# Output steps of ssm and mlstm in three overlapping parts with stated places in all queues; s5 scan of layer 1 behind both units of mlstm inputs

## The chip, the cores and the metric

One core of one Trainium2 chip runs the whole program. The metric is the device time of one execution in microseconds. The engines are TensorE (PE, matmuls; PEld is its weight load), VectorE (DVE), ScalarE (ACT), GpSimd (POOL) and SyncE (SP, which issues all transfers here). Each takes its instructions in the order in which they were queued at build time, and an instruction whose inputs are not there holds up what stands behind it in the same queue.

## The reference

The reference is a two-layer backbone on a context of 256 tokens and a latent of 256 tokens, width 1024, float32. Each layer is: SwiGLU block, a mixing stage, SwiGLU block, each behind a root-mean-square norm with shift and scale. The mixing stage projects the tokens with one wide matrix and feeds four branches. Two of them matter here, and a third gives way to them:

```python
def ssd_scan(xs, dt, bm, cm, a, h0):            # "ssm", 8 heads, chunks of 128, two directions
    decay = jnp.exp(masked_diff(g, False))      # g: cumulative sum of dt*a in a chunk
    scores = einsum('bcihn,bcjhn->bchij', cq, bq) * decay
    y_intra = einsum('bchij,bcjhp->bcihp', scores, x*dt)
    y_inter = einsum('bcihn,bcih,bchnp->bcihp', cq, exp(g), h_prev)
    return y_intra + y_inter
def mlstm_scan(q, k, v, ig, lf, state):         # "ml", 4 heads, two directions
    w_intra = exp(dmat - m_out) * einsum('bcihk,bcjhk->bchij', qq, kq)
    num = w_intra @ v + w_x * (q @ c_prev)
    den = max(|sum(w_intra) + w_x * (q @ n_prev)|, exp(-m_out))
    return num / den
# "s5": a complex diagonal recurrence over time; "gdn": a gated delta rule with a triangular inverse per chunk
# merge: sum over branches of gate * (y @ w_branch), then @ w_out
```

Layer 0 needs outputs for both segments (four chunks of 128 tokens), layer 1 for the latent alone (two chunks, 2 and 3), though its states run over all four.

## The kernel before, in words

Matmuls of the projections run in three passes of a split weight. `weights` (L360) loads a tile of 512 KB on SP's queue (`w_dma`), ACT casts it to the high part (L366, `w_cast`), DVE forms the low part (L371, `w_split`); the float tile, the high part and the low part have three buffers each. `proj` (L384) runs the three matmuls of a product (L380, L381, L382): a projection of 256 output columns over 512 tokens is two weight tiles and 48 matmuls; over 256 tokens the matmuls have half as many columns. This is called a unit below.

The mixing stage `mix` takes its steps from a string, `MIX_ORDER` (L1708), one per layer. Steps that are one unit of projection: `q0 q2 v0 v1` (inputs of ml), `c0` to `c6` (inputs of ssm), `i0` to `i10` (inputs of gdn), `oM`, `zS`, `zG` (gates of ml, ssm and gdn), `ga1` to `gd3` (merge gates; branch 0 is ssm, 1 ml, 2 s5, 3 gdn). `rows`, `ml`, `ssm`, `s5` and `gdn` are generators; `ssm:1` runs one part, up to its next `yield`. The units between the parts give PE work while other engines prepare.

The order of instructions in each queue is found by a planner at build time, which follows data dependences, buffers and its own estimate of durations. The string sets its preferences, and a mark sets a lower bound: with `'` the step's PE instructions come behind the last matmul of the steps traced before; with `!` its instructions come behind that matmul, behind the last weight cast on ACT, the last split on DVE and the last weight load on SP:

```python
f, behind = f.lstrip("'!"), {"'": 1, "!": 4}.get(f[0], 0)
for h in (self.last_mm, self.w_cast, self.w_split, self.w_dma)[:behind]:
    st.enter_context(self.tc.issue_after(h.ins))
```

The string is taken apart at L1782 and the marks are read at L1849. Before, nearly all output parts of ml and ssm have the mark `'`.

`ssm` (L846): transposes, then a part with the chunk states, then one part per chunk, then the final norm. A chunk takes each direction in turn: SP loads the row tile (`spread`, L742: 8 rows of `rowd` to all 128 partitions, 512 KB); ACT (L910) and DVE (L912) form the differences; ACT takes the Exp (L914, L916); DVE multiplies by the masked scores (L918, L923) and POOL by the C inputs (L925); PE runs the products (L930), and DVE adds the skip (L934). The row tile and E sit in buffer slots 8 and 0, one per direction.

`ml` (L958): load and transposes, states, then one part per chunk, then the norm. A chunk loads 16 rows (1 MB) into slot 7, clamps eight of them on DVE (L1014), takes Exp on ACT (L1015), scores on PE (L1021), masks and weighs on DVE (L1027, L1030, L1036), and runs the products on PE (L1042, L1047); DVE and ACT divide (L1050 to L1058).

`s5_scan` (L1593): U is loaded from `dU` by eight transfers (L1555), PE forms the inputs of the recurrence (L1606), ACT and DVE lay them out (L1614, L1615), and POOL runs 63 steps of four instructions each (L1620 to L1623). `s5` later reads the result (first product L1662). `gdn`'s inverse is a loop of 31 steps on DVE and POOL (L1114, L1116); PE's first matmul after it is L1150.

Of the kernel before, what the change touches and what calls it, by code (L numbers as in the profile page):

```python
# [747 lines left out]
class Ssm:  # L748
# [97 lines left out]
    def ssm(self, l, P, G, o0, dz):  # L846
# [45 lines left out]
        yield  # L892

        y = xs
        for c in range(o0, 4):
# [2 lines left out]
            for g in range(2):
                nc.tensor.matmul(pS[:, g * 128:(g + 1) * 128], lhsT=bc[:, g, sl], rhs=bc[:, 2 + g, sl], start=True, stop=True)
            py = self.ps()  # L900
            nj = sum(1 + ((d, c) in Hs) for d in range(2))
            j = 0
            for d in range(2):
                eg = self.t8((8, 0)[d], [128, 2, 8, 128])
                E, gb = eg[:, 0], eg[:, 1]
                self.spread(gb, d * 8, 8, c)
                for h in range(8):
                    g = G["g"][:, c, d, h:h + 1]
                    if h < 4:
                        nc.scalar.activation(E[:, h], gb[:, h], AF.Relu, scale=-1.0, bias=g)  # L910
                    else:
                        ts(E[:, h], gb[:, h], g, 0.0, op0=OP.subtract, op1=OP.min)  # L912
                inter = (d, c) in Hs
                nc.scalar.activation(E[:, 0:4], E[:, 0:4], AF.Exp, scale=-1.0)  # L914
                e_ = eg.rearrange("p t h i -> p (t h) i")[:, 4:8 + 8 * inter]
                nc.scalar.activation(e_, e_, AF.Exp)  # L916
                Sm, xd = self.k2([128, 2, 128]), self.k2([128, 8, 64])
                tt(Sm, pS[:, 0:256].rearrange("p (g i) -> p g i", g=2),  # L918
                   self.tri[:, d].unsqueeze(1).to_broadcast([128, 2, 128]), op=OP.mult)
                tt(xd, xt[:, c], b8(G["dt"][:, c, d], 64), op=OP.mult)  # L920
                for g in range(2):
                    hs = slice(g * 4, g * 4 + 4)
                    tt(E[:, hs], E[:, hs], Sm[:, g].unsqueeze(1).to_broadcast([128, 4, 128]), op=OP.mult)  # L923
                    if inter:
                        nc.gpsimd.tensor_tensor(gb[:, hs], gb[:, hs], bc[:, 2 + g, sl].unsqueeze(1).to_broadcast([128, 4, 128]), op=OP.mult)  # L925
# [1037 lines left out]
```

## Time and profile before

| | us |
|---|---|
| median of three runs | 2853.37 (2846.23 to 2858.15) |
| the profiled execution | 2849.91 |
| its span, first to last instruction | 2848.2 |
| PE busy | 2710.5 (95%) |
| DVE busy | 1724.6 (61%) |
| ACT busy | 1110.8 (39%) |
| POOL busy | 730.6 (26%) |

The profile is one execution. Busy time is the time in which an engine runs an instruction; idle time before an instruction is put down to what released it last. The granted clock is 1.00 at 2.4 GHz and 0.50 at 1.2 GHz; a stretch that saw both has a mean in between. The mixing stage of layer 0 lies at about 480 to 1240 us of the span, that of layer 1 at about 2080 to 2640.

### The profile page before, as it was taken

How to read it: one execution, taken by the hardware profiler on the slowest of the kernel's cores; microseconds unless marked ns; L12 is line 12 of the kernel's file. 1: busy time of each engine (PE TensorE's matmuls, PEld its weight loads, DVE VectorE, ACT ScalarE, POOL GpSimd, SP SyncE). 2: the span in 40 equal slices, each digit the busy share in tenths (PEclk: the TensorE clock that was granted, in tenths of full speed). 3: DMA queues.
4: the chain of work that ended last, by engine and by line, in shares of the span. 5: the costliest groups of instructions: out<-in, count | busy, mean ns of one | idle time of the engine just before them, and what ended most of it. 6: DMA issues, size and time to landing. Idle time of an engine off the chain costs nothing.

```text
span 2848.2 us, 46282 instructions
## 1 busy us (share of the span) xinstructions
PE 2710.5 (95%) x17710; PEld 2278.2 (80%) x17710; DVE 1724.6 (61%) x3234; ACT 1110.8 (39%) x1711; POOL 730.6 (26%) x1129
## 2 busy tenths in 40 slices
PE   7999999898989999999999999999989998969999
PEld 5777679687867888897678897778978878869999
DVE  6664346477965665674333476554565996766655
ACT  4322224444544533242212353222445456623443
POOL 1442001493021331520000014420107901434100
PEclk9999999999998999999999999999999998979999
DMA  8444878555555544667662353443475557754564
GB/s 269 121 152 132 272 271 216 145 158 153 178 155 174 165 132 152 207 204 260 228 225 89 110 158 121 134 151 106 145 192 168 167 185 237 223 153 129 168 189 144
DMA packets 509819, 494.18 MB, mean 174 GB/s; under 512 B 79380, under 2 KB 437838, under 8 KB 508574
## 3 DMA queue, kind: packets, MB, share of 16 engines
q1 hardware_dynamic: 509598, 491.22, 56.2%
q8 instruction: 140, 2.29, 0.3%
q14 instruction: 81, 0.66, 0.1%
HBM read 429.17 MB, written 61.96 MB: 172 GB/s over the span
## 4 chain that ended last, share of the span: by engine, by line
PE 79%; DVE 6%; DMA 6%; issue 3%; ACT 2%; POOL 2%; SPq 1%; DVEq 0%; POOLq 0%; ACTq 0%
PE ffn.pb L380 15%; PE ffn.pb L381 15%; PE ffn.pb L382 15%; PE gates.pb L381 2%; PE gates.pb L380 2%; PE gates.pb L382 2%; PE ffn.ps L187 2%; DMA ssm.t<-rows.rowd 2%; PE merge.pb L380 1%; PE merge.pb L381 1%; PE merge.pb L382 1%; PE gdnin.pb L382 1%; PE gdnin.pb L381 1%; PE gdnin.pb L380 1%; PE mlin.pb L452 1%
## 5 line engine op out<-in xcount | busy, mean ns | idle before, releaser
L371 DVE TENSOR_TENSOR ffn.wl<-ffn.wf,ffn.wh 128x1024 fp32r<-128x1024 f32 (+1 forms) x308 | 370.3, 1202 | 377.4 <-ACT ffn.wh L366 367.5
L366 ACT CAST ffn.wh<-ffn.wf 128x1024 fp32r<-128x1024 f32 (+1 forms) x308 | 310.4, 1008 | 556.0 <-PE ffn.pb L382 398.6
L382 PE MATMUL ffn.pb<-ffn.t,ffn.wh 128*128 128x256 f32 (+1 forms) x1312 | 438.5, 336 | 0.0
L381 PE MATMUL ffn.pb<-ffn.t,ffn.wl 128*128 128x256 f32 (+1 forms) x1312 | 438.3, 336 | 0.0
L380 PE MATMUL ffn.pb<-ffn.t,ffn.wh 128*128 128x256 f32 (+1 forms) x1312 | 434.7, 338 | 1.0 <-ACT ffn.t L344 1.0
L380 PEld LDWEIGHTS ffn.pb<-ffn.t,ffn.wh 128*128 128x128 f32 x1312 | 244.1, 189 | 34.2 <-ACT ffn.wh L366 4.2
L382 PEld LDWEIGHTS ffn.pb<-ffn.t,ffn.wh 128*128 128x128 f32 x1312 | 246.5, 188 | 29.8 <-issue 2.4
L381 PEld LDWEIGHTS ffn.pb<-ffn.t,ffn.wl 128*128 128x128 f32 x1312 | 247.3, 189 | 28.3 <-issue 1.6
L380 PE MATMUL ffn.pb<-wout.t,ffn.wh 128*128 128x256 f32 (+1 forms) x720 | 242.5, 338 | 0.9 <-ACT wout.t L344 0.9
L381 PE MATMUL ffn.pb<-wout.t,ffn.wl 128*128 128x256 f32 (+1 forms) x720 | 241.4, 336 | 0.0
L382 PE MATMUL ffn.pb<-wout.t,ffn.wh 128*128 128x256 f32 (+1 forms) x720 | 239.2, 335 | 0.0
L381 PE MATMUL gates.pb<-ffn.t,gates.wl 128*128 128x512 f32 (+1 forms) x512 | 178.8, 350 | 5.7 <-DVE gates.wl L371 5.7
L380 PE MATMUL gates.pb<-ffn.t,gates.wh 128*128 128x512 f32 (+1 forms) x512 | 177.1, 348 | 1.9 <-ACT zs.kf L807 1.8
L382 PE MATMUL gates.pb<-ffn.t,gates.wh 128*128 128x512 f32 (+1 forms) x512 | 176.5, 346 | 0.0
L313 POOL TENSOR_TENSOR norm.kf<-norm.kf,norm.kf 128x256 f32<-128x256 f32 x45 | 41.5, 923 | 518.8 <-ACT norm.kf L311 508.4
L380 PEld LDWEIGHTS ffn.pb<-wout.t,ffn.wh 128*128 128x128 f32 x720 | 137.5, 191 | 26.5 <-ACT ffn.wh L366 7.5
L381 PEld LDWEIGHTS ffn.pb<-wout.t,ffn.wl 128*128 128x128 f32 x720 | 136.1, 189 | 16.2 <-issue 0.8
L382 PEld LDWEIGHTS ffn.pb<-wout.t,ffn.wh 128*128 128x128 f32 x720 | 135.1, 189 | 16.0 <-issue 0.8
L380 PE MATMUL ffn.pb<-t,ffn.wh 128*128 128x512 f32 x352 | 142.2, 404 | 2.1 <-DVE ffn.kf L493 1.9
L381 PE MATMUL ffn.pb<-t,ffn.wl 128*128 128x512 f32 x352 | 142.1, 404 | 0.0
L382 PE MATMUL ffn.pb<-t,ffn.wh 128*128 128x512 f32 x352 | 139.3, 401 | 0.0
L381 PEld LDWEIGHTS gates.pb<-ffn.t,gates.wl 128*128 128x128 f32 x512 | 99.8, 195 | 17.9 <-DVE gates.wl L371 6.3
(583 smaller groups left out, 6279.4 us busy)
## 6 DMA issues: line engine op xcount, KB each, us to landing
ffn.wf<-in_ffn_up_dram SPq DMA_DIRECT2D x176, 512.0 KB
ffn.t<-in_ada_w_dram SPq DMA_DIRECT2D x68, 1024.0 KB
ffn.wf<-in_ffn_down_dram SPq DMA_DIRECT2D x104, 512.0 KB
gates.wf<-in_w_in_dram SPq DMA_DIRECT2D x64, 512.0 KB
merge.wf<-in_w_branch_dram SPq DMA_DIRECT2D x32, 512.0 KB
zs.wf<-in_w_in_dram SPq DMA_DIRECT2D x24, 512.0 KB
gdnin.wf<-in_w_in_dram SPq DMA_DIRECT2D x24, 512.0 KB
wout.wf<-in_w_out_dram SPq DMA_DIRECT2D x24, 512.0 KB
```

The source lines that it names most:

```text
L187: nc.tensor.matmul(pm[32 * k:32 * k + 32, :], lhsT=self.sF[:, h * 4 + k, 28 - 4 * i:60 - 4 * i], rhs=ws[h][:, k], start=(h == 0), stop=(h ...
L313: nc.gpsimd.tensor_tensor(sq[0], sq[0], q, op=OP.add)
L366: self.w_cast = nc.scalar.copy(wh[:, :nk, :nw], wf[:, :nk, :nw])
L371: self.w_split = nc.vector.tensor_tensor(wl[:, :nk, :nw], wf[:, :nk, :nw], wh[:, :nk, :nw].bitcast(F32), op=OP.subtract)
L380: mm(out, lhsT=ah, rhs=bh, start=start, stop=False)
L381: mm(out, lhsT=al, rhs=bh, start=False, stop=False)
L382: self.last_mm = mm(out, lhsT=ah, rhs=bl, start=False, stop=stop)
L452: self.last_mm = self.nc.tensor.matmul(o, lhsT=a, rhs=b[:, k], start=(k0 + k == 0 and i == 0 and c % 2 == 0), stop=(k0 + k == nK - 1 and i ...
```

## The change

Three edits. In `ssm`, one output run is now one chunk and direction (eight runs in layer 0, four in layer 1). `rows(i)` sends run i's row transfer into slot 8 or 0 in turn, `prepare(i)` does the work of ACT, DVE and POOL and the scores, `products(i)` runs PE's products and, after the second direction, the skip. A part of the generator is `products(i-1)`, `rows(i+1)`, `prepare(i)`; the first two row transfers stand in the part with the states. In `ml` the same split is made by chunk, with the rows in slots 7 and 0 in turn; the weighed queries are written into the row tile itself. In `MIX_ORDER` the output parts of ml and all but the first parts of ssm get the mark `!`, nearly every part has a unit of projection behind it, in layer 0 more of the merge gates stand ahead of `s5` (ssm has four more parts there, and two more in layer 1), and in layer 1 `s5scan` stands behind `q0` in place of in front of it. The diff is cut: the lines that only move are left out where the new function repeats them.

```diff
@@ -889,50 +889,76 @@
                     tt(Hn, Hs[d, c], b8(G["et"][:, c, d, 0:8], 64), op=OP.mult)
                     tt(Hn, Hn, pv, op=OP.add)
                 Hs[d, ORDER[d][i + 1]] = Hn
-        yield
+
 
         y = xs
-        for c in range(o0, 4):
+        runs = [(c, d) for c in range(o0, 4) for d in range(2)]
+        egs, have, ops = {}, {}, {}
+
+        def rows(i):
+            if i < len(runs):
+                c, d = runs[i]
+                egs[i] = self.t8((8, 0)[i % 2], [128, 2, 8, 128])
+                self.spread(egs[i][:, 1], d * 8, 8, c)
+
+        def prepare(i):
+            c, d = runs[i]
             sl = slice(c * 128, (c + 1) * 128)
-            pS = self.ps()
+            eg = egs.pop(i)
+            E, gb = eg[:, 0], eg[:, 1]
+            for h in range(8):
+                g = G["g"][:, c, d, h:h + 1]
+                if h < 4:
+                    nc.scalar.activation(E[:, h], gb[:, h], AF.Relu, scale=-1.0, bias=g)
+                else:
+                    ts(E[:, h], gb[:, h], g, 0.0, op0=OP.subtract, op1=OP.min)
+            inter = (d, c) in Hs
+            nc.scalar.activation(E[:, 0:4], E[:, 0:4], AF.Exp, scale=-1.0)
+            e_ = eg.rearrange("p t h i -> p (t h) i")[:, 4:8 + 8 * inter]
+            nc.scalar.activation(e_, e_, AF.Exp)
+            if d == 0:
+                pS = have["S"] = self.ps()
+                for g in range(2):
+                    nc.tensor.matmul(pS[:, g * 128:(g + 1) * 128], lhsT=bc[:, g, sl], rhs=bc[:, 2 + g, sl], start=True, stop=True)
+            Sm, xd = self.k2([128, 2, 128]), self.k2([128, 8, 64])
+            tt(xd, xt[:, c], b8(G["dt"][:, c, d], 64), op=OP.mult)
+            tt(Sm, have["S"][:, 0:256].rearrange("p (g i) -> p g i", g=2),
+               self.tri[:, d].unsqueeze(1).to_broadcast([128, 2, 128]), op=OP.mult)
             for g in range(2):
...
-            j = 0
-            for d in range(2):
-                eg = self.t8((8, 0)[d], [128, 2, 8, 128])
-                E, gb = eg[:, 0], eg[:, 1]
-                self.spread(gb, d * 8, 8, c)
+                hs = slice(g * 4, g * 4 + 4)
+                tt(E[:, hs], E[:, hs], Sm[:, g].unsqueeze(1).to_broadcast([128, 4, 128]), op=OP.mult)
+                if inter:
+                    nc.gpsimd.tensor_tensor(gb[:, hs], gb[:, hs], bc[:, 2 + g, sl].unsqueeze(1).to_broadcast([128, 4, 128]), op=OP.mult)
+            ops[i] = ((xd, E), (Hs.get((d, c)), gb))[:1 + inter]
+
+        def products(i):
+            c, d = runs[i]
+            sl = slice(c * 128, (c + 1) * 128)
+            if d == 0:
+                have["y"], have["j"] = self.ps(), 0
+            py = have["y"]
+            nj = sum(1 + ((e, c) in Hs) for e in range(2))
+            for a, b in ops.pop(i):
+                j = have["j"]
                 for h in range(8):
...
-                for a, b in ((xd, E), (Hs.get((d, c)), gb))[:1 + inter]:
-                    for h in range(8):
...
+                    k, e = h // 2, h % 2
+
+                    nc.tensor.matmul(py[e * 64:e * 64 + 64, k * 128:(k + 1) * 128], lhsT=a[:, h], rhs=b[:, h],
+                                     start=(j == 0 and k == 0), stop=(j == nj - 1), skip_group_check=True)
+                have["j"] += 1
+            if d:
+                for k in range(4):
+                    stt(y[:, k, sl], xs[:, k, sl], P["ssm_d"][:, k:k + 1], py[:, k * 128:(k + 1) * 128], op0=OP.mult, op1=OP.add)
+        rows(0)
+        rows(1)
+        yield
+        for i in range(len(runs) + 1):
+            if i:
+                products(i - 1)
+                rows(i + 1)
+            if i < len(runs):
+                prepare(i)
+                yield
@@ -1002,12 +1028,19 @@
                     tt(Cn, Cn, pv, op=OP.add)
                 Cp = Cn
                 Cs[d, ORDER[d][i + 1]] = Cn
-        yield
+
+
         h_ = self.t8(6, [128, 4, 4, 128])
         ss = self.keep("mss", [128, 4, 4])
-        for c in range(o0, 4):
+        rws, ops = {}, {}
+
+        def rows(c):
+            if c < 4:
+                rws[c] = self.spread(self.t8((7, 0)[c % 2], [128, 16, 128]), 24, 16, c)
+
+        def prepare(c):
             sl = slice(c * 128, (c + 1) * 128)
-            rw = self.spread(self.t8(7, [128, 16, 128]), 24, 16, c)
...
-            rd = self.k2([128, 2, 4])
-            pns = []
+            ops[c] = []
...
                 w = rw[:, d * 4:d * 4 + 4]
                 tt(w, w, Sm, op=OP.mult)
-                qw = None
                 if (d, c) in Cs:
-                    qw = self.k2([128, 2, 128])
                     for e in range(2):
                         q = slice(e * 64, e * 64 + 64)
-                        tt(qw[q], qk[q, 0:2, sl], rw[q, 8 + d * 4 + e:8 + d * 4 + 4:2], op=OP.mult)
+                        qw = rw[q, 8 + d * 4 + e:8 + d * 4 + 4:2]
+                        tt(qw, qk[q, 0:2, sl], qw, op=OP.mult)
+                ops[c].append((w, rw[:, 8 + d * 4:12 + d * 4] if (d, c) in Cs else None))
+
+        def products(c):
+            rd = self.k2([128, 2, 4])
+            for d, (w, qw) in enumerate(ops.pop(c)):
                 pn = [self.ps() for _ in range(2)]
-                pns.append(pn)
...
-                        nc.tensor.matmul(dst(h), lhsT=qw[q, k], rhs=Cs[d, c][q, k], start=False, stop=True, skip_group_check=True)
+                        nc.tensor.matmul(dst(h), lhsT=qw[q, h], rhs=Cs[d, c][q, k], start=False, stop=True, skip_group_check=True)
...
-            yield
+        rows(o0)
+        rows(o0 + 1)
+        yield
+        for c in range(o0, 5):
+            if c > o0:
+                products(c - 1)
+                rows(c + 1)
+            if c < 4:
+                prepare(c)
+                yield
...
 MIX_ORDER = (
-    "rows:1 load s5in oM0 s5scan rows:1 oM2 loc q2 q0 v0 v1 ml:2 c0 'ml:1 c2 'ml:1 c4 'ml:1 c6 'ml:1 zS0 zS2 'ml:1 i4 "
-    "'ssm:1 i6 'ssm:1 i8 'ssm:1 i10 'ssm:1 i2 'ssm:1 i0 'ssm:1 ga1 'ssm:1 !s5:1 gb1 's5:1 gc1 s5:1 gdn:1 gd1 gdn:1 ga2 "
-    "gdn:6 glu gb2 gc2 gd2 ga0 gb0 gc0 gd0 zG0 zG2 ga3 !gdn:1 gb3 'gdn:6 gc3 gd3 out m1 m2 m3 m0",
-    "load rows:1 s5in q2 s5scan q0 'rows:1 v0 loc v1 oM0 oM2 ml:2 c0 'ml:1 c2 'ml:1 c4 c6 ml:1 zS0 'ssm:1 zS2 i4 'ssm:1 "
-    "i6 'ssm:1 i8 'ssm:1 i10 'ssm:1 !s5:1 i0 i2 's5:1 zG0 s5:1 zG2 gdn:1 ga2 gdn:1 gb2 gdn:6 "
+    "rows:1 load s5in oM0 s5scan rows:1 oM2 loc q2 q0 v0 v1 ml:2 c0 !ml:1 c2 !ml:1 c4 !ml:1 c6 !ml:1 zS0 !ml:1 zS2 "
+    "'ssm:1 i4 'ssm:1 i6 !ssm:1 i8 !ssm:1 i10 !ssm:1 i2 !ssm:1 i0 !ssm:1 ga1 !ssm:1 gb1 !ssm:1 gc1 !ssm:1 gd1 !ssm:1 "
+    "!s5:1 ga2 's5:1 gb2 s5:1 gdn:1 gc2 gdn:1 gd2 gdn:6 ga0 glu gb0 gc0 gd0 zG0 zG2 !gdn:1 ga3 gb3 'gdn:6 gc3 gd3 "
+    "out m1 m2 m3 m0",
+    "load rows:1 s5in q2 q0 s5scan 'rows:1 v0 loc v1 oM0 oM2 ml:2 c0 !ml:1 c2 !ml:1 c4 c6 !ml:1 zS0 'ssm:1 zS2 "
+    "'ssm:1 i4 !ssm:1 i6 !ssm:1 i8 !ssm:1 i10 !ssm:1 i0 !ssm:1 !s5:1 i2 's5:1 zG0 s5:1 zG2 gdn:1 ga2 gdn:1 gb2 gdn:6 "
     "gc2 glu gd2 ga1 gb1 gc1 gd1 ga0 gb0 gc0 gd0 !gdn:1 ga3 gb3 'gdn:6 gc3 gd3 out m2 m1 m3 m0",
 )
```

## Rows read from the trace of the kernel before

**Rows 1.** The page's first table: engine, busy us, share, instructions.

```profile
PE 2710.5 (95%) x17710; PEld 2278.2 (80%) x17710; DVE 1724.6 (61%) x3234; ACT 1110.8 (39%) x1711; POOL 730.6 (26%) x1129
```

**Rows 2.** Stretches 480:1260 and 2060:2680, sum and mean: busy us by engine.

```profile
sum 1400.00, PE 1287.49 PEld 1130.64 DVE 969.57 ACT 638.67 POOL 514.03; mean PE 643.74 PEld 565.32 DVE 484.78 ACT 319.33 POOL 257.01
```

**Rows 3.** PE's timeline, layer 0, q0: start, us, instruction, [idle before <-its end].

```profile
558.24 0.39 PE L381 MATMUL mlin.pb<-ffn.t,mlin.wl 128*128 128x512 f32 x1
558.47 0.40 PE L382 MATMUL mlin.pb<-ffn.t,mlin.wh 128*128 128x512 f32 x1
...
564.02 0.79 PE L380 MATMUL mlin.pb<-ffn.t,mlin.wh 128*128 128x512 f32 x1 [5.15 <-ACT mlin.wh L366]
```

**Rows 4.** ACT's timeline, the same place.

```profile
555.86 1.28 ACT L910 ACTIVATE ssm.t<-ssm.t,rows.gc 128x128 f32<-128x128 f32 x4 [5.08 <-DMA ssm.t<-rows.rowd]
...
562.94 1.03 ACT L366 CAST mlin.wh<-mlin.wf 128x1024 fp32r<-128x1024 f32 x1
```

**Rows 5.** Stretches: length, busy us of PE, PEld, DVE, ACT, POOL; clock, DMA, GB/s.

```profile
560.00:572.00 12.00, 7.51 (x20) 5.63 (x21) 8.64 (x18) 8.93 (x14) 11.21 (x21) 0.72 0.24 69
679.00:691.00 12.00, 5.09 (x24) 4.10 (x23) 10.29 (x22) 3.12 (x4) 2.66 (x2) 0.72 0.56 180
...
2120.00:2140.00 20.00, 12.07 (x222) 11.71 (x222) 12.30 (x28) 7.48 (x18) 2.04 (x6) 0.74 0.79 127
2170.00:2182.00 12.00, 5.92 (x25) 5.42 (x25) 3.70 (x8) 9.87 (x18) 10.82 (x32) 0.72 0.54 173
...
2518.00:2558.00 40.00, 20.88 (x409) 20.34 (x409) 21.60 (x53) 8.31 (x13) 10.84 (x10) 0.57 0.30 84
```

**Rows 6.** Timelines of PE and ACT, layer 1, at the scan and at oM.

```profile
2127.93 0.87 PE L1606 MATMUL s5scan.ps<-s5scan.t,s5scan.t 128*64 128x64 f32 x11 [8.13 <-DMA s5scan.t<-prep.s5K]
...
2169.18 1.28 ACT L910 ACTIVATE ssm.t<-ssm.t,rows.gc 128x128 f32<-128x128 f32 x4 [4.71 <-DMA ssm.t<-rows.rowd]
...
2175.03 0.58 PE L380 MATMUL zs.pb<-ffn.t,zs.wh 128*128 128x256 f32 x1 [5.28 <-ACT zs.wh L366]
```

**Rows 7.** Timelines of SP, DVE, PE around ml's third chunk, layer 0.

```profile
666.47 0.39 SPq L742 DMA_DIRECT2D ml.t<-rows.rowd  x1
...
677.97 0.48 DVE L1014 TENSOR_SCALAR ml.t<-ml.t,rows.gmc 128x128 f32<-128x128 f32 x2 [6.56 <-DMA ml.t<-rows.rowd]
...
686.22 2.07 PE L1042 MATMUL ml.ps<-ml.k,ml.t 128*128 128x130 f32 x8 [6.91 <-issue]
```

**Rows 8.** PE's waits, 800:860: instruction, releaser: us in total, times, longest.

```profile
PE ssm.ps L930 <- DVE ssm.t L923: 7.5, 8, 1.8
PE ssm.ps L930 <- POOL ssm.t L925: 1.2, 2, 0.8
```

**Rows 9.** PE's waits, 2200:2364, first and last of eight.

```profile
PE zs.pb L381 <- DVE zs.wl L371: 4.5, 2, 2.9
...
PE ml.ps L1070 <- DVE ml.t L1066: 0.6, 1, 0.6
```

**Rows 10.** POOL's timeline, layer 1, ssm's first multiplies.

```profile
2274.01 6.48 POOL L925 TENSOR_TENSOR ssm.t<-ssm.t,ssm.t 128x512 f32<-128x512 f32 x4
```

**Rows 11.** PE's groups by line, 2317.6:2376.6: xcount | busy, mean ns | idle.

```profile
L381 PE MATMUL gates.pb<-ffn.t,gates.wl 128*128 128x256 f32 x38 | 12.9, 338 | 0.0
...
L930 PE MATMUL ssm.ps<-ssm.t,ssm.k 128*64 128x128 f32 x64 | 4.8, 280 | 1.4 <-DVE ssm.t L923 1.4
```

**Rows 12.** Stretches inside the scan of layer 1, columns as in rows 5.

```profile
2160.00:2170.00 10.00, 9.76 (x83) 9.55 (x82) 2.41 (x6) 4.88 (x11) 8.90 (x27) 1.00 0.59 161
2220.00:2230.00 10.00, 10.00 (x59) 8.22 (x58) 9.86 (x21) 5.31 (x11) 9.38 (x16) 1.00 0.61 141
```

**Rows 13.** SP's waits at L742, whole span: durations in ns, min/median/max.

```profile
L742 SPq EVENT_SEMAPHORE  x19: 17/17/1423, 534.8 to 2331.4; - x19
```

**Rows 14.** The chain of waits, 790:860: start, us, piece.

```profile
809.20 8.53 DMA ssm.t<-rows.rowd
```

**Rows 15.** PE's timeline behind the gdn inverse, layer 1.

```profile
2535.42 1.27 PE L1150 MATMUL gdn.ps<-gdn.k,gdn.t 32*32 32x32 f32 x20 [16.78 <-DMA gdn.k<-gdn.gz]
```

More of the change, by code (lines that the diff above doesn't have):

```diff
@@ L891, in ssm @@
                 Hs[d, ORDER[d][i + 1]] = Hn
-        yield
-        y = xs
-        for c in range(o0, 4):
-            sl = slice(c * 128, (c + 1) * 128)
-            pS = self.ps()
[L898 to L901, printed above, removed]
-            j = 0
-            for d in range(2):
-                eg = self.t8((8, 0)[d], [128, 2, 8, 128])
-                E, gb = eg[:, 0], eg[:, 1]
-                self.spread(gb, d * 8, 8, c)
-                for h in range(8):
[L908 to L925, printed above, removed]
-                for a, b in ((xd, E), (Hs.get((d, c)), gb))[:1 + inter]:
-                    for h in range(8):
-                        k, e = h // 2, h % 2
-                        nc.tensor.matmul(py[e * 64:e * 64 + 64, k * 128:(k + 1) * 128], lhsT=a[:, h], rhs=b[:, h],
-                                         start=(j == 0 and k == 0), stop=(j == nj - 1), skip_group_check=True)
-                    j += 1
-            for k in range(4):
-                stt(y[:, k, sl], xs[:, k, sl], P["ssm_d"][:, k:k + 1], py[:, k * 128:(k + 1) * 128], op0=OP.mult, op1=OP.add)
-            yield
@@ new lines, in ssm @@
+        y = xs
+        runs = [(c, d) for c in range(o0, 4) for d in range(2)]
[28 more added lines that the diff above has]
+               self.tri[:, d].unsqueeze(1).to_broadcast([128, 2, 128]), op=OP.mult)
+            for g in range(2):
+                hs = slice(g * 4, g * 4 + 4)
[3 more added lines that the diff above has]
+            ops[i] = ((xd, E), (Hs.get((d, c)), gb))[:1 + inter]
@@ new lines, in products @@
+        def products(i):
+            c, d = runs[i]
+            sl = slice(c * 128, (c + 1) * 128)
+            if d == 0:
[4 more added lines that the diff above has]
+                j = have["j"]
+                for h in range(8):
+                    k, e = h // 2, h % 2
[5 more added lines that the diff above has]
+                    stt(y[:, k, sl], xs[:, k, sl], P["ssm_d"][:, k:k + 1], py[:, k * 128:(k + 1) * 128], op0=OP.mult, op1=OP.add)
@@ L1004, in ml @@
                 Cs[d, ORDER[d][i + 1]] = Cn
-        yield
         h_ = self.t8(6, [128, 4, 4, 128])
         ss = self.keep("mss", [128, 4, 4])
-        for c in range(o0, 4):
+        rws, ops = {}, {}
[3 more added lines that the diff above has]
+        def prepare(c):
             sl = slice(c * 128, (c + 1) * 128)
-            rw = self.spread(self.t8(7, [128, 16, 128]), 24, 16, c)
+            rw = rws.pop(c)
             for d in range(2):
```

## The prediction

> **What bounds the kernel now.** The table of engines comes first: TensorE (PE) is busy for 95% of the span [rows 1]. A change that takes no matmul away can only win what PE idles or runs at its lower clock. The table of stretches over the two mixing stages, the only code the diff touches, says how much that is: of 1400 us PE is busy for 1287.5, so 112.5 us are idle; the next engine, VectorE, is busy for 969.6 [rows 2]. The list of PE's waits and the timelines then say which of these belong to edited steps.
>
> The most telling one: PE stops for 5.15 us until ScalarE (ACT) has cast a weight tile [rows 3]. ACT's timeline shows why. ACT stood 5.08 us at a Relu of the state-space step, for a transfer from `rowd`, and the cast came only after that step's Exp [rows 4]. The state-space output step was hoisted there, in front of the mLSTM step, because its place was stated in PE's queue alone. After such a stop the granted clock falls to 1.2 GHz: the stretch around it has a mean of 0.72 [rows 5], so 12 x 0.28 = 3.4 us of full-speed work are lost.
>
> **The change, part by part.** Counted in the code, no matmul, elementwise instruction or transfer is added or removed: there are still 12 row transfers for ssm and 6 for ml. What changes is when each may issue.
>
> *Stated places in all queues.* Layer 0's hoisted Relus now stand behind a weight cast of the gdn inputs, so the stop above goes: 5.15 + 3.4 = 8.6 us; I take 8.5, since the same ACT work lands later, beside projections. Layer 1 has the twin: ACT stands 4.71 us at the same Relu and PE 5.28 us at the cast behind it [rows 6], with a mean clock of 0.72 again [rows 5]: 8.7, taken 8.5.
>
> *Row tiles in two buffers, products one unit after their preparation.* Today one buffer holds ml's rows, so the transfer for the next chunk issues only after the products that read the old one. SyncE (SP) issued it at 666.47, VectorE (DVE) stood 6.56 us for it until 677.97, and PE stood 6.91 us for what DVE makes of it [rows 7]. The transfer thus took 11.5 us. A projection unit (48 matmuls, 0.23 us apart [rows 3]) lasts 11.3 us. With two buffers the transfer issues one unit earlier and PE comes to the products one unit later, so this wait has about two units of cover. Worth 6.91 plus half of 12 x 0.28 (the rest of the low clock fell into the wait): 8.6, taken 8.
>
> In ssm of layer 0, PE waits 7.5 + 1.2 = 8.7 us, ten times, for what DVE and GpSimd (POOL) multiply for the step it wants at once [rows 8]. A unit of cover removes these; I take 6, because DVE and ACT still stand at row transfers and may be late once or twice.
>
> *s5scan of layer 1 behind q0.* PE waits 8.13 us for transfers before the scan's matmuls [rows 6]. q0 there has 256 columns, half a unit, so 5.6 us of matmuls slide into the gap. The stretch has a mean clock of 0.74 [rows 5], 5.2 us lost, half of which falls into the wait: 5.6 + 2.6 = 8.2. The weights of q0 must be issued by the same SP queue that is busy with the scan's own transfers, so I take 6.
>
> *The rest of layer 1.* From 2200 to 2364 the wait list has eight rows that sum to 13.6 us, from 4.5 down to 0.6 [rows 9]: splits and casts late behind ml and ssm work. I take 6: part of it is transfers and sums that do not move.
>
> Upper bound 8.6 + 8.7 + 8.6 + 8.7 + 8.2 + 13.6 = 56.4; lower bound, if only the two hoisted Relus go, 17; taken 8.5 + 8.5 + 8 + 6 + 6 + 6 = 43.
>
> *What the change costs.* In layer 1 POOL runs the scan until 2274.01, and only then ssm's first four multiplies, 6.48 us [rows 10]. Before, ssm's products all ran after 2317, behind i8 and i10 [rows 11], so this cost nothing. The places now put i8 and i10 (22.6 us) behind the first products, and layer 1's gains take up to 20 us off: 2317 - 43 = 2274, when POOL is just free and needs 3.2 us for the first pair. I charge 4. It costs more if the scan is slower, and it is slower beside a busy DVE: with DVE busy 2.41 of 10 us POOL runs 27 instructions, with 9.86 it runs 16 [rows 12]. The 252 instructions of a scan (63 steps of four) take 93 us at the one rate and 158 at the other; if all of it moved to the lower one, layer 1's gain would be gone (third rival). The Trainium skill, "SBUF — State Buffer", section "Who interferes with whom", has the rule that speaks against this change: a VectorE instruction with two SBUF inputs and a GpSimd instruction that reads SBUF exclude each other for the whole instruction. The trace agrees, with the 27 against 16 instructions above.
>
> SP: a transfer into a reused buffer waits in SP's queue for the products; behind it stand the weight loads of the next units. The wait before such a transfer was at most 1.4 us [rows 13], and weights have three buffers of half a unit each, so nothing to 14 us over ten such transfers, taken 0. DVE and ACT: behind a Relu or clamp that waits stand the next unit's cast and split. A 512 KB transfer takes 8.5 us [rows 14], less than a unit, so I take 0; the other end is the second rival.
>
> Sum: 43 - 4 = 39 us. The profiled execution took 2849.9 us (span 2848.2 and 1.7 around it), 3.5 below the median of 2853.4; from the median, **2814 us**.
>
> **Rivals.**
>
> 1. *The end of layer 1 is covered as well.* PE waits 16.78 us for the gdn inverse [rows 15], and the mean clock there is 0.57 [rows 5]: 40 x 0.43 = 17 us, of which about 8 fall on work. For: the order text has s5 ahead of all gates, yet 38 x 3 = 114 gate matmuls, 2.4 units, ran before s5's first product [rows 11], since ml and ssm were late. If these steps keep their places, s5 and gdn start earlier against the projections that cover the inverse. Against: DVE runs the inverse as well and splits the same weights. 25 us more: 2789. Chance 0.20.
>
> 2. *Slower: the stated place makes DVE and ACT stand at a row transfer.* Ten transfers cannot be sent before their loop (2 of ml, 6 of ssm in layer 0, 2 of ssm in layer 1). Each is sent when products end, and its reader has a place behind the last cast and split of the next unit, which can run up to half a unit ahead of PE. If the place comes first, everything behind it stalls as in [rows 3]: 5.15 + 3.4 = 8.6 us. Eight times (the ssm ones) are 69: 2814 + 69 = 2883. It outweighs the gain from the fifth such stop on. For: 11.5 us measured for the larger transfer is no less than a unit. Against: ssm's 8.5 is less, and weights already split keep PE going. Chance 0.12. The Trainium skill, "DMA: Bandwidth & Descriptors", section "Bandwidth", gives 6.15 us for 1 MB loaded into 128 partitions from GpSimd's queue, about half of the 11.5 us that the 1 MB row transfer took here. By that figure all ten would be covered and this rival void; the trace disagrees, so it stays.
>
> 3. *Layer 1 hands its part back*, to the scan on POOL or to a longer wait at the inverse. Of 43, the 20.5 of layer 1 go with the 4 charged: 2814 + 16.5 = 2830. For: DVE and POOL, not PE, pace that stretch. Chance 0.13.
>
> 4. *It does not do what it says.* A place is a lower bound and the instruction order between the places is found by a planner, so waits may move by a unit without getting shorter: the 114 matmuls ahead of s5 show how far the real order drifts from the text [rows 11]. 2853. Chance 0.13.
>
> **How the numbers follow.** Forecast 0.42, rivals 0.20, 0.12, 0.13, 0.13. The forecast's own range is 2797 (56.4 of gain) to 2836 (the hoisted Relus alone). From 2775 to 2862 the range holds the forecast, the third and fourth rivals and most of the first; it leaves out the second and a little at each end, some 0.18. A change within 0.5% (14.3 us) is what a measurement here cannot tell from none. Faster: 0.41 + 0.20 + 0.12 = 0.73. Slower: the second rival, 0.12. The same: 0.15.
>
> **What would show it.** PE's waits for `mlin.wh` at layer 0's q0 and for `zs.wh` at layer 1's oM0 are gone, and ACT has no ssm Relu before ml's first chunk. The 6.91 us ahead of ml's products is gone, and ml's clamps wait less for `rowd`. The wait ahead of the scan's matmuls in layer 1 is under 3 us. POOL's first ssm multiply of layer 1 follows the scan without a pause (then the scan is the new bound there); with a pause, the 4 us were not paid. s5's product of layer 1 comes before the gates: then the 16.78 us shrink. I am wrong if PE's idle time in the two stages stays near 112 us, or if casts wait behind ssm Relus inside the ssm stretch.

## The result and the profile after

The changed kernel takes 2810.13 us (median of four runs, 2805.00 to 2820.62) against 2855.76 us for the kernel before beside it: ratio 0.9849, 95% interval 0.9811 to 0.9888. A second set gave 2811.46 against 2850.83: 0.9868, 0.9854 to 0.9883. So it is faster by 1.3 to 1.5%, and 2814 us had been predicted. The profiled execution took 2805.0 us.

The first table of the page after, which answers to [rows 1]:

```profile
PE 2687.4 (96%) x17710; PEld 2258.2 (81%) x17710; DVE 1729.0 (62%) x3234; ACT 1114.1 (40%) x1711; POOL 748.3 (27%) x1129
```

The number of instructions is the same on every engine; PE is busy for 23 us less. Where both come from is seen by cutting each trace at the same work: layer 0's mixing stage from the first matmul of its `rows` step to the last of the output projection, layer 1's from the first matmul of ml's inputs to the last of the output projection. First the kernel before, then the kernel after, in the columns of [rows 5]:

```profile
478.00:1263.00 785.00, 744.06 (x4738) 624.01 (x4738) 519.01 (x1012) 338.24 (x535) 267.03 (x404) 0.97 0.56 166
2103.00:2643.00 540.00, 472.78 (x4097) 439.42 (x4095) 401.03 (x821) 260.33 (x439) 235.79 (x385) 0.92 0.62 181
```

```profile
478.00:1242.00 764.00, 734.48 (x4741) 617.61 (x4741) 524.82 (x1013) 339.84 (x534) 270.02 (x404) 0.98 0.58 170
2082.00:2606.00 524.00, 466.88 (x4098) 433.77 (x4096) 400.74 (x821) 261.62 (x440) 249.79 (x385) 0.93 0.64 186
```

Layer 0 is 21 us shorter: idle time falls from 785 - 744.1 = 40.9 to 29.5 us, and the busy time for the same matmuls by 9.6 us, with the mean clock up from 0.97 to 0.98. Layer 1 is 16 us shorter: 10.1 of idle time and 5.9 of busy time. The part between the two stages took 840.15 us in both. The remaining 7.6 us of the two profiles lie in the last SwiGLU block, which the change does not touch (below).

At layer 0's q0, the place of [rows 3] and [rows 4], the same 40 us before and after:

```profile
550.00:590.00 40.00, 34.38 (x207) 30.19 (x207) 24.55 (x40) 20.60 (x36) 37.02 (x76) 0.91 0.53 156
```

```profile
550.00:590.00 40.00, 40.00 (x272) 36.79 (x271) 25.65 (x43) 16.42 (x24) 37.10 (x75) 1.00 0.68 194
```

PE does 272 matmuls in place of 207, all at full clock. At ml's third chunk, which answers to [rows 7], DVE's clamp of the changed kernel still stands for its rows. PE's next products belong to the second chunk, since products now run one unit late, and wait 1.76 us in place of 6.91; this is the only wait of PE ahead of ml's output products in that layer:

```profile
629.83 0.43 DVE L1047 TENSOR_SCALAR ml.t<-ml.t,rows.gmc 128x128 f32<-128x128 f32 x1 [6.14 <-DMA ml.t<-rows.rowd]
```

```profile
641.10 1.13 PE L1077 MATMUL ml.ps<-ml.k,ml.t 128*128 128x130 f32 x8 [1.76 <-DVE ml.t L1062]
```

Layer 1's gains and its remaining stops show in PE's waits from the start of its stage (waiting instruction, releaser: us in total, times, longest), which answer to [rows 6]:

```profile
PE s5scan.ps L1650 <- DMA s5scan.t<-prep.s5K: 4.6, 1, 4.6
PE zs.pb L380 <- ACT zs.wh L366: 3.1, 1, 3.1
PE ml.ps L1020 <- DVE ml.k L1016: 2.9, 1, 2.9
PE rows.ps L716 <- DVE s5scan.t L1659: 2.2, 1, 2.2
PE zs.pb L381 <- DVE zs.wl L371: 0.9, 1, 0.9
```

8.13 us at the scan have become 4.6, and the stop at oM's cast and split is 3.1 + 0.9 in place of 5.3 + 1.3. ACT's timeline says that it has another cause now: ACT stands for the load of ml's own queries and keys, no longer for ssm's rows.

```profile
2147.21 0.63 ACT L992 ACTIVATE ml.t<-ml.t 128x512 f32<-128x512 f32 x1 [15.10 <-DMA ml.t<-ffn.mlqk]
```

How little that start of the stage gained is seen by cutting layer 1 at the same place and at s5's first product. The kernel before, then the kernel after:

```profile
2103.00:2200.00 97.00, 82.05 (x813) 75.03 (x813) 53.40 (x121) 46.40 (x87) 50.84 (x136) 0.91 0.70 180
2200.00:2376.60 176.60, 162.97 (x1056) 141.38 (x1052) 160.71 (x316) 94.27 (x152) 86.95 (x142) 0.95 0.61 184
```

```profile
2082.00:2180.00 98.00, 84.11 (x840) 76.05 (x839) 55.58 (x130) 43.82 (x79) 51.28 (x132) 0.97 0.73 189
2180.00:2337.70 157.70, 150.33 (x966) 130.58 (x964) 154.01 (x301) 92.69 (x153) 101.72 (x146) 0.95 0.60 181
```

PE idles 15.0 us in the first 97 us of the stage before and 13.9 in the first 98 after; from there to s5's first product it is 13.6 and 7.4.

The wait behind the gdn inverse of [rows 15] is where it was:

```profile
2498.83 3.43 PE L1194 MATMUL gdn.ps<-gdn.k,gdn.t 32*32 32x32 f32 x64 [16.46 <-DMA gdn.k<-gdn.gz]
```

### The profile page after: what moved, and what is told of

Its sections match the earlier page's. It is cut to its first block, busy times and chain, and to the rows that moved or that the text cites. A ratio compares the mean times of both kernels' runs of the same rounds, so it can differ in the third digit from the quotient of the medians.

```text
span 2803.3 us, 46292 instructions
## 1 busy us (share of the span) xinstructions
PE 2687.4 (96%) x17710; PEld 2258.2 (81%) x17710; DVE 1729.0 (62%) x3234; ACT 1114.1 (40%) x1711; POOL 748.3 (27%) x1129
## 4 chain that ended last, share of the span: by engine, by line
PE 50%; DVE 9%; issue 4%; DMA 4%; POOL 2%; ACT 1%; SPq 1%; DVEq 0%; POOLq 0%; ACTq 0%
PE ffn.pb L380 11%; PE ffn.pb L381 11%; PE ffn.pb L382 11%; PE gates.pb L380 2%; PE gates.pb L381 2%; PE gates.pb L382 2%; PE ffn.ps L187 1%; PE merge.pb L382 1%; PE merge.pb L380 1%; PE merge.pb L381 1%; DVE gdnin.kf L790 1%; PE wout.pb L382 1%; PE wout.pb L381 1%; PE wout.pb L380 1%; DVE ssmin.kf L790 1%
## 5 line engine op out<-in xcount | busy, mean ns | idle before, releaser
L493 DVE SCALAR_TENSOR_TENSOR ffn.kf<-ffn.kf,ffn.pb 128x512 f32<-128x512 f32 (+1 forms) x88 | 54.6, 620 | 94.8 <-ACT ffn.kf L491 94.8
```

The source lines that it names most:

```text
L493: nc.vector.scalar_tensor_tensor(g[:, :n], t[:, :n], 1.0, p, op0=OP.add, op1=OP.mult)
```

## The experiments

All lengths are of one profiled execution each, cut as above; "last" is from there to the end of the span.

| kernel | median us | ratio to before (95%) | layer 0 | layer 1 | last |
|---|---|---|---|---|---|
| before | 2855.8 | | 784.7 | 540.1 | 205.1 |
| before, again (e13) | 2852.3 | 1.0000 (0.9986 to 1.0015) | 788.4 | 534.5 | 198.2 |
| changed | 2810.1 | 0.9849 (0.9811 to 0.9888) | 763.3 | 524.1 | 197.5 |
| changed, again (e4) | 2811.5 | 0.9868 (0.9854 to 0.9883) | 766.8 | 525.2 | 197.6 |
| e1: no places | 2827.4 | 0.9920 (0.9904 to 0.9935) | 776.3 | 526.8 | 198.7 |
| e2: places, old code | 2852.6 | 1.0007 (0.9992 to 1.0021) | 785.0 | 546.7 | 197.7 |
| e3: scan first | 2811.9 | 0.9862 (0.9841 to 0.9883) | 770.3 | 524.2 | 198.3 |
| e5: ml alone | 2819.5 | 0.9893 (0.9869 to 0.9917) | 766.7 | 531.5 | 199.0 |
| e6: ssm alone | 2833.4 | 0.9937 (0.9916 to 0.9959) | 778.5 | 534.4 | 198.7 |
| e7: ml behind its gate | 2801.6 | 0.9835 (0.9809 to 0.9860) | 762.6 | 517.2 | 198.4 |
| e9: short scan | 2808.1 | 0.9849 (0.9821 to 0.9878) | 762.2 | 528.4 | 197.6 |
| e10: ssm free | 2821.6 | 0.9895 (0.9878 to 0.9911) | 766.2 | 531.6 | 198.9 |
| e11: ml free | 2829.6 | 0.9918 (0.9901 to 0.9934) | 782.6 | 526.6 | 205.6 |
| e12: ml behind each unit | 2819.7 | 0.9887 (0.9873 to 0.9902) | 766.9 | 532.2 | 198.8 |

The changed kernel, its repeat, e3, e7, e9 and e12 have the same order of steps in layer 0 and lie between 762.2 and 770.3 there. The two profiles of the kernel before differ by 3.7 us in layer 0 and 5.6 in layer 1. A difference of less than some 8 us in layer 0 or 6 us in layer 1 is therefore not read as one, unless a wait in the trace shows it.

**e4, e13: each kernel again.** No edit.

> The changed kernel once more, nothing altered. The last 205 us of the program before (the second SwiGLU block of layer 1, which the change does not touch) took 7.6 us less in the profile of the changed kernel, with the 256-column matmuls 113.3 ns apart in place of 117.8 at the same granted clock of 1.00. Theory P (the pace belongs to the kernel): 197.5 us again there, mixing stages of 763 and 524 us within 1 us. Theory R (the pace is an accident of the execution): the stretch, or another with 256 columns in layer 1, comes out at the other pace, up to 7.6 us away, and the mixing stages move by no more than their own matmuls' pace.

> The kernel before once more. Its profile had 784.7 and 540.1 us in the mixing stages and 205.1 us in the last SwiGLU block, where eight other profiles, one of them of old code, had 197.5 to 199. Theory R (that pace is an accident of one execution): 197.5 to 199 us this time, the mixing stages within 4 us of 784.7 and 540.1. Theory P (the pace belongs to this program): 205 us again.

Theory R held. The kernel before has 198.2 us in its last block the second time, and e11 is the only other one at 205. The rest of the spread is in the stages. In this second pair PE idles 44.8 and then 29.9 us in layer 0, 64.8 and then 54.9 in layer 1, so the gain of idle time is there again. Of the busy time, layer 0 gains again (743.6 to 737.1 us), layer 1 does not (469.7 to 470.4).

**e1: the places taken away.** In every output part of ml and ssm:

```diff
-c0 !ml:1 c2 !ml:1 c4 !ml:1 c6 !ml:1 zS0 !ml:1
+c0 'ml:1 c2 'ml:1 c4 'ml:1 c6 'ml:1 zS0 'ml:1
...
-i6 !ssm:1 i8 !ssm:1 i10 !ssm:1
+i6 'ssm:1 i8 'ssm:1 i10 'ssm:1
```

> The changed kernel with the places of the ml and ssm output parts stated in PE's queue alone again; the two buffers, the lag of one unit and the order of steps stay. Theory A (the places make the hoisted ScalarE work wait its turn): ScalarE's ssm Relus go back in front of the weight casts at layer 0's q0 and at layer 1's oM, PE stops there again for about 5 us each, and with the low clock each mixing stage is 8 to 9 us longer (layer 0 from 763 to about 772, layer 1 from 524 to about 532): about 2827 us. Theory B (the gain comes from the two buffers and the lag; the places are idle): both stages within 2 us of the changed kernel, about 2810 us.

Measured: 2827.43, theory A to the microsecond. But the split over the layers is not A's: layer 0 loses about 11 us and layer 1 about 2, no more than its spread. And the stop at q0 is not a copy of the old one. It ends with VectorE, not with ACT's cast, and ACT stands three times around it, 8.44 us for ml's Exp, 4.48 for ssm's Relu and 5.26 for ml's second Exp, so theory A has only part of the cause:

```profile
566.01 0.79 PE L381 MATMUL mlin.pb<-ffn.t,mlin.wl 128*128 128x512 f32 x1 [5.98 <-DVE mlin.kf L783]
```

In layer 1 PE stops at oM for 6.9 + 2.3 us in place of 3.1 + 0.9, and the stage is still only 2 us longer. Buffers, lag and order alone thus keep 23 of the 39 us that the changed kernel gained beside the same runs of the kernel before (2850.83); the places are worth the other 16. What each of buffers, lag and order is worth was not tested by itself, except for the scan's place (e3).

**e2: the places given to the old code.**

```diff
-c0 'ml:1 c2 'ml:1 c4 'ml:1 c6 'ml:1 zS0 zS2 'ml:1 i4 'ssm:1
+c0 !ml:1 c2 !ml:1 c4 !ml:1 c6 !ml:1 zS0 zS2 !ml:1 i4 !ssm:1
```

> The kernel before with the places of its ml and ssm output parts stated in all four queues, nothing else. Theory A: the two hoisted stops go (8.5 us in each stage: layer 0 from 785 to about 776, layer 1 from 540 to about 531), while the 6.9 us ahead of ml's products and the 8.7 us of ssm's small waits in layer 0 stay: about 2836 us. Theory B: nothing is gained, about 2855 us, since a part that is prepared and used in one step now also starts later. Theory D (places without the lag cost): DVE and ACT do everything for a product only after the unit's casts, PE waits longer at each ml and ssm product, and the kernel is slower than before, 2865 us or more.

Theory A missed by 17 us: nothing was gained. The stop at q0 is gone here too (PE runs its four ml input units in 45.28 us, as in the changed kernel, in place of 53.95), yet the stage is as long as before. PE's waits from 790 to 870 us, next to [rows 8], show where it went:

```profile
PE ssm.ps L930 <- DVE ssm.t L923: 8.7, 8, 2.1
PE ssm.ps L283 <- ACT ssm.k L839: 7.0, 1, 7.0
PE ssm.ps L930 <- POOL ssm.t L925: 3.9, 5, 1.1
```

8.7 us of waits for the operands of a step have become 8.7 + 3.9, and 7.0 more stand ahead of the norm. A part that is prepared and used in one step, and may not start early, is late when PE comes to it. Layer 1 is even longer, 546.7 us against 540.1 and 534.5. So the places gave nothing without the rest of the change; the rest gave 23 us without the places (e1).

**e3: the scan in front of q0 again.**

```diff
-s5in q2 q0 s5scan 'rows:1
+s5in q2 s5scan q0 'rows:1
```

> The changed kernel with layer 1's s5 scan in front of q0 again. Theory A: PE waits about 8.1 us ahead of the scan's matmuls in place of 4.6, and layer 1's mixing stage is 4 to 6 us longer (524 to about 529): about 2815 us. Rival (GpSimd's scan is what bounds ssm there): the scan starts and ends some 5 us earlier, ssm's first multiplies too, and layer 1's stage is the same or shorter: 2805 to 2810 us.

Measured: 2811.93, and 524.2 us in layer 1, as with the scan behind q0. PE's waits at the start of the stage:

```profile
PE s5scan.ps L1650 <- DMA s5scan.t<-prep.s5K: 9.6, 1, 9.6
PE ml.ps L1020 <- DVE ml.k L1016: 3.6, 1, 3.6
PE ssmin.pb L381 <- DVE ssmin.wl L371: 0.8, 1, 0.8
```

The wait at the scan is longer, 9.6 us, but the 3.1 at oM's cast and the 2.2 behind the scan are not there: in the first 98 us of the stage 4.6 + 3.1 + 2.9 + 2.2 + 0.9 = 13.7 stand against 9.6 + 3.6 + 0.8 = 14.0. The stop moved; it was not covered.

**e5 and e6: ml's part alone, ssm's part alone.** Each takes one generator from the change with its places (e6 with layer 0's later order too) and leaves the other, and the scan, as before.

```diff
 e5
-c0 'ml:1 c2 'ml:1 c4 'ml:1 c6 'ml:1 zS0 zS2 'ml:1 i4 'ssm:1
+c0 !ml:1 c2 !ml:1 c4 !ml:1 c6 !ml:1 zS0 !ml:1 zS2 i4 'ssm:1
 e6
-zS2 'ml:1 i4 'ssm:1 i6 'ssm:1 i8 'ssm:1
+zS2 'ml:1 'ssm:1 i4 'ssm:1 i6 !ssm:1 i8 !ssm:1
```

> From the kernel before, ml's part of the change alone: two row buffers, products one unit late, places of ml's parts in all queues; ssm's code, places and order and the scan's place as before. Theory A (the parts add up): ml gives its 8 us of layer 0 (785 to about 777) and 3 to 5 us in layer 1 (540 to about 536), the stop at q0 stays since ssm's Relus are still free to go ahead: about 2840 us. Theory J (the parts work only together, as the places without the lag gave nothing): under 4 us in all, about 2848 us.

> From the kernel before, ssm's part of the change alone: one chunk and direction per part, products one unit late, places in all queues, layer 0's later order; ml and the scan's place as before. Theory A (the parts add up): the stop at layer 0's q0 and its twin in layer 1 go, and the small waits of ssm too: layer 0 from 785 to about 772, layer 1 from 540 to about 529: about 2826 us. Theory J: under 8 us in all, about 2843 us or more.

ml alone gives 30 us, over twice what theory A had for it, and 18 to 22 of them in layer 0: within the spread, the whole of that layer's gain. ssm alone gives 16 us. The two sum to 46 us and both take away the stop at q0, so their gains overlap; it counts once in the whole. The stop is absent in both; the same 40 us as above, e5 and then e6:

```profile
550.00:590.00 40.00, 40.00 (x273) 36.77 (x272) 26.58 (x44) 18.57 (x30) 37.17 (x73) 1.00 0.64 189
```

```profile
550.00:590.00 40.00, 40.00 (x259) 36.19 (x258) 26.16 (x44) 17.27 (x26) 37.18 (x73) 1.00 0.66 194
```

In e5 ssm's Relu still goes ahead on ACT and stands there for 9.41 us, and PE does not stop; in e6 it is ml's Exp, which stands for 7.84 us. The line of e5:

```profile
552.88 1.29 ACT L910 ACTIVATE ssm.t<-ssm.t,rows.gc 128x128 f32<-128x128 f32 x4 [9.41 <-DMA ssm.t<-rows.rowd]
```

The twin in layer 1 parts the two. In e5 it is gone, with ssm's Relu standing 7.64 us on ACT. In e6, where ssm's Relus have their place, it stays, and ACT stands twice for ml (PE's waits at oM, then ACT's timeline ahead of the casts):

```profile
PE zs.pb L380 <- ACT zs.wh L366: 6.3, 1, 6.3
PE zs.pb L381 <- DVE zs.wl L371: 0.7, 1, 0.7
```

```profile
2155.30 1.06 ACT L1041 ACTIVATE ml.t<-ml.t 128x1024 f32<-128x1024 f32 x1 [9.06 <-DVE ml.t L1040]
...
2168.31 0.63 ACT L992 ACTIVATE ml.t<-ml.t 128x512 f32<-128x512 f32 x1 [8.95 <-DMA ml.t<-ffn.mlqk]
```

**e10 and e11: one of the two freed in the changed kernel.** The marks of ssm (e10) or of ml (e11) are `'` again, as in e1.

> The changed kernel with the places of the ssm output parts stated in PE's queue alone; ml's stay in all queues. Without any of these places layer 0's stage took 776 us, with all of them 763 to 770. Theory A (as predicted: the hoisted ssm Relus on ScalarE stop PE at q0): PE stops about 5 us at q0 again, layer 0's stage about 775 us, layer 1's 527: about 2825 us. Theory M (ml's clamps on VectorE and Exp on ScalarE, waiting there for their own rows, make the stop; the ssm Relu alone is covered by weights already split, as with ml's part alone, where ScalarE stood 9.41 us for it and PE ran on): no stop at q0, layer 0's stage within 763 to 771 us: about 2812 us.

> The changed kernel with the places of the ml output parts stated in PE's queue alone; ssm's stay in all queues. Theory A: no stop at q0, since the ssm Relus keep their place: 763 to 771 us in layer 0's stage, about 2812 us. Theory M: the stop of 5 to 6 us at q0 is back, with VectorE standing at ml's clamps for the second chunk's rows, and layer 0's stage takes about 775 us: about 2823 us.

Theory M held for layer 0, though e11's stage is longer still than its 775 us (782.6; the four ml input units took 54.7 us in place of 45.3). PE's 40 us at q0, e10 and then e11:

```profile
550.00:590.00 40.00, 40.00 (x272) 36.74 (x271) 24.30 (x37) 18.58 (x30) 37.10 (x75) 1.00 0.72 200
```

```profile
550.00:590.00 40.00, 33.39 (x179) 28.57 (x178) 24.51 (x48) 15.13 (x21) 36.86 (x82) 0.87 0.52 159
```

In e10 ACT stands 9.31 us for ssm's rows, ahead of a cast, and the casts and splits already done carry PE over it. In e11 no ssm work stands ahead; ml's does. Its clamps wait on DVE and its Exp behind them on ACT, twice, since two row buffers let the second chunk come forward as well (DVE, then ACT):

```profile
567.78 1.99 DVE L1047 TENSOR_SCALAR ml.t<-ml.t,rows.gmc 128x128 f32<-128x128 f32 x8 [12.16 <-issue]
569.69 1.34 DVE L371 TENSOR_TENSOR mlin.wl<-mlin.wf,mlin.wh 128x1024 fp32r<-128x1024 f32 x1
```

```profile
553.92 1.06 ACT L1048 ACTIVATE ml.t<-ml.t 128x1024 f32<-128x1024 f32 x1 [8.26 <-DVE ml.t L1047]
...
569.81 1.06 ACT L1048 ACTIVATE ml.t<-ml.t 128x1024 f32<-128x1024 f32 x1 [12.43 <-DVE ml.t L1047]
```

The median of e10, 2821.57, is still 10 us above the changed kernel: its layer 1 is 7 us longer, in one profile. That part theory M did not foresee. The traces place it: s5's first product comes 257.0 us after the stage's start, as in the changed kernel (256.0 and 257.7), and from there to the first matmul behind the gdn inverse it is 166.0 us in place of 161.1 and 160.0. What makes that stretch longer stays open.

**e9: half of the scan.** Layer 1's scan runs 31 of its 63 steps; the later half of that recurrence is left out.

```diff
-        for n in range(1, 64):
+        for n in range(1, 32 if l else 64):
```

> The changed kernel with 31 of the 63 steps of layer 1's s5 scan on GpSimd, which leaves the later half of that recurrence out. In the changed kernel the scan runs from 2127 to 2266 and ssm's first multiplies follow it without a pause. Theory S (the scan bounds ssm's output part, and with it all that follows in layer 1, for at least the 4 us charged): the multiplies come 40 us or more earlier and layer 1's stage of 524 us is shorter by 4 to 20 us. Rival (the multiplies have slack, their products have a later place): they come earlier, the products do not, and the stage stays within 2 us of 524. A faster DVE beside a quiet GpSimd would give up to 2 us more in both.

Counted from the start of the stage, POOL ends the scan 83 us earlier, stands for 55 us, and begins ssm's multiplies 28 us earlier. First the last scan instruction and the first multiplies of e9, then the first multiplies of the changed kernel, which follow its scan at once:

```profile
2181.05 0.50 POOL L1667 TENSOR_TENSOR s5scan.t<-s5scan.s5m 128x64 f32<-128x64 f32 x1
2236.68 3.39 POOL L931 TENSOR_TENSOR ssm.t<-ssm.t,ssm.t 128x512 f32<-128x512 f32 x2 [55.13 <-ACT gdnin.wh L366]
```

```profile
2266.17 6.79 POOL L931 TENSOR_TENSOR ssm.t<-ssm.t,ssm.t 128x512 f32<-128x512 f32 x4
```

Layer 1 is not shorter: 528.4 us against 524.1 and 525.2, and s5's first product comes 256.3 us after the stage's start, against 256.0 and 257.7. The length of the scan bounds nothing there.

**e7 and e12: a better order for layer 1.**

```diff
 e7
-oM0 oM2 ml:2 c0 !ml:1 c2 !ml:1 c4 c6 !ml:1
+oM0 !ml:1 oM2 !ml:1 c0 !ml:1 c2 !ml:1 c4 c6 !ml:1
 e12
+oM0 oM2 !ml:1 c0 !ml:1 c2 !ml:1 c4 !ml:1 c6 !ml:1
```

> The changed kernel with layer 1's first two parts of ml given places too: the first behind the first unit of ml's gate, the second behind the second unit. In the changed kernel ScalarE stands 15.10 us there for ml's load from memory ahead of a weight cast, and PE stops 3.13 us. Theory A (same cause as the hoisted Relus): that stop goes and with it some clock, layer 1's stage 3 to 5 us shorter (525 to about 521): about 2807 us. Rival (ml's states are then late): PE waits 3 us or more for ml's first transposes or states in its place, and nothing is gained: 2811 us or more.

> A version meant to beat the changed kernel: in layer 1 each of ml's five parts stands behind one unit (the first behind both units of its gate, then one behind each of the four units of ssm's inputs), all in all queues. Giving the first two parts places one unit earlier took layer 1's stage from 524 to 517 us. Theory A (every part behind its own unit, the loads of ml have a unit more): PE's wait of 3.27 us for ml's values goes too, layer 1's stage 513 to 517 us, about 2799 us. Rival (ml's last part and so ssm's transposes come a unit later, and the chain from ssm to the inverse with them): 520 to 528 us, about 2808 us.

e7 is the fastest of all: 2801.64 us (2798.84 to 2808.39), and layer 1 takes 517.2. It was timed beside the kernel before, not beside the changed one, whose eight runs lie between 2805.00 and 2820.62 us, and the intervals of the two ratios overlap; that it beats that one too rests on the stage, 7 us shorter in one profile, little more than the spread. PE's waits at the start of its stage:

```profile
PE s5scan.ps L1650 <- DMA s5scan.t<-prep.s5K: 5.2, 1, 5.2
PE ml.ps L1020 <- DMA ml.k<-ffn.mlv: 3.3, 1, 3.3
PE rows.ps L716 <- DVE s5scan.t L1659: 2.0, 1, 2.0
```

The wait for oM's cast is gone, 3.1 + 0.9 us, and ACT stands for ml's load for 1.12 us in place of 15.10. Both theories had part of it: a wait of 3.3 for ml's values takes the place, and what is won shows later, in a first s5 product 247.8 us after the stage's start in place of 256.0. That the stop alone was worth 7 us is not shown: e3 is without it too, and e1 has more than twice of it, and their stages are within 3 us of the changed kernel's. e12, one unit later, loses it all and more: 532.2 us, worse than its rival's 520 to 528. PE's last matmul of ml ends there at 171 us of the stage, against 158 in e7, and its first of ssm starts at 182 against 169. Of the 15 us between the two stages 8.5 are there at s5's first product (256.3 us) and 5 more come between it and the inverse.

## Why the prediction was right, and where it was not

**The stop at layer 0's q0, 8.5 us: right size, half the cause.** It went: PE's four ml input units take 45.28 us in place of 53.95, 8.7 less. But "The state-space output step was hoisted there" is not the whole reason. In the kernel before ACT stood twice in a row, for ml's clamped rows and then for ssm's (the second is the line of [rows 4]):

```profile
548.27 1.06 ACT L1015 ACTIVATE ml.t<-ml.t 128x1024 f32<-128x1024 f32 x1 [7.99 <-DVE ml.t L1014]
```

Taking out either one suffices (e5, e6). In the new code, where two row buffers let ml's second chunk come forward, it is ml's place that matters (e11) and ssm's that does not (e10). Where ACT stood once there, for 7.8 to 9.4 us (e5, e6, e10), the weights already split carried PE over it; where it stood for 13 us or more in all (before, e1, e11), PE stopped.

**Its twin in layer 1, 8.5 us: wrong.** The ssm Relu left, and ACT then stood 15.10 us in the same place for ml's own load, whose part has no mark. 3.1 + 0.9 us of PE's stop of 5.3 + 1.3 stayed. The step failed by naming the releaser of a wait as its cause, without asking what else stood unplaced in ACT's queue. In the kernel before that was ml's Exp, 9.34 us ahead of the Relu's 4.71: with ssm's places alone the stop stays (6.3 + 0.7, e6), with ml's it goes (e5). In the changed kernel it is ml's load: with a place for that part too, the stop goes (e7). It goes as well with the scan in front (e3), where ACT stands 10.68 us for the same load.

**ml's row buffers, 8 us: right, a little low.** ml alone, with its places, buffers and lag, takes 18.0 to 21.6 us off layer 0 (against the two profiles of before); without the 8.7 to 9.7 of the stop at q0, 9 to 12 remain.

**ssm's small waits in layer 0, 6 us: too much.** From 770 to 850 us PE still waits 3.7 + 1.8 = 5.5 us for the same operands, in place of 8.7:

```profile
PE ssm.ps L946 <- DVE ssm.t L929: 3.7, 5, 2.3
PE ssm.ps L946 <- POOL ssm.t L931: 1.8, 2, 1.5
```

That is 3.2 us, with 2.0 more for two waits ahead of ssm's norm that are gone, and layer 0 with ml's part alone (766.7) is already as short as with both (762.2 to 770.3). DVE and ACT still stand at ssm's row transfers in layer 0: ACT for 23.2 us in five waits, in place of 36.9 in six.

**The scan behind q0, 6 us: wrong.** e3 has it at nothing. q0 covers part of the transfers' time, and the stop returns one step later. Together the twin and the scan counted on 5.28 + 5.6 = 10.9 us less idle time at the start of the stage. PE idles 15.0 and 16.0 us there in the two profiles of before, 13.9 and 12.9 in the two of the changed kernel: about 2 us less. Its mean clock there was 0.91 in both of before, and 0.97 and 0.91 after, so no gain of clock is shown.

**The rest of layer 1, 6 us: right.** The waits of [rows 9] sum to 13.6 us (10.7 in the second profile of before); their successors, from 2180 to s5's first product at 2337.7, to 7.1 (7.3 in the second profile). That is 3.5 to 6.5 us.

**The scan on POOL, a cost of 4 us: not paid.** By the prediction's own test, multiplies without a pause behind the scan, it would have been. e9 shows that the test was a poor one: work that follows another without a pause sets the time only if someone waits for it, and in the changed kernel PE never waits for POOL's multiplies in layer 1 (its waits at these products, 1.1 us, are for DVE).

**The rivals.** *The end of layer 1 covered*: 16.46 us stand in place of 16.78. 54 gate matmuls instead of 114 ran ahead of s5's first product, so more cover was left, and it did not reach the inverse. From s5's first product to the first matmul behind the inverse it is 158.8 us before and 161.1 after, with 60 matmuls more (7 us) in it. PE's idle time in that stretch fell from 32.0 to 28.7 us (31.1 to 27.7 in the second profiles), so the end was covered a little better, but not at the inverse. *DVE and ACT standing at row transfers*: they do, and outside ssm's own products PE stops for it at one place in layer 0, 3.49 us at zS, behind a clamp that waits 3.67. The 8.53 us that the prediction read for a 512 KB transfer is not the longest in that chain of the kernel before: another took 12.12 us from its issue, over a unit. *Layer 1 hands its part back*: no. *It does not do what it says*: not for the change, but it is just what the places do by themselves (e2).

**The sum.** 22.5 us were predicted for layer 0; the means of the two profiles of each kernel differ by 786.5 - 765.0 = 21.5. 16.5 were predicted for layer 1; they differ by 537.3 - 524.7 = 12.6. 34 of the 39 us were there. Layer 0 came out by its steps, except that ssm's waits gave less and ml's buffers more. Layer 1 came near by luck: two terms of 14.5 us had about 2 us of idle time behind them, and two errors the other way made up for part of it, the cost of 4 that was not paid and the 3.3 us less idle time between s5 and the inverse, which no term counted. Between the medians lie 39 to 46 us. The rest is as large as the pace of the last block and the spread of single executions, so it is not ascribed to a step.

## What to carry to other kernels

A place stated in more queues calls for a lag between preparing and using: given to code without lag and second buffer it won nothing here, while lag, buffers and order won 23 us without the places and the places 16 more on top. Before naming an instruction as the one that holds up a queue, take it and its neighbours out one at a time, since another unplaced one may stand there too or take its place. And "B starts the moment A ends" makes A the bound only if something waits for B.
